# Feed-forward operands without 1/rms for the early batches alone, then rebuilt from DRAM

## The chip, the cores and the metric

The kernel runs on one core of a Trainium2 chip. The metric is device microseconds of one execution. Five engines work side by side: PE (matrix products; PEld are its weight loads), DVE (element-wise work), ACT (functions and copies), POOL (element-wise work, SBUF only) and SP, whose queue issues all the DMAs of this kernel. PE's clock is granted at one of two levels, 2.4 or 1.2 GHz.

## The reference, cut to what matters

Two layers; each is a token mixer followed by a SwiGLU feed-forward block, S = 1024 tokens, D = 1024, F = 2816:

```python
h = rms_norm(x, ffn_norm_g[layer])       # x * rsqrt(mean(x*x) + eps) * g
a = einsum('bsd,df->bsf', h, w_gate)
u = einsum('bsd,df->bsf', h, w_up)
x = x + einsum('bsf,fd->bsd', silu(a) * u, w_down)
```

The change lies in the two gate-and-up stages, `a` and `u`.

## The kernel before, in words

Tokens lie along the free dimension, in two halves `th` of 512; features lie on the 128 partitions. Every float32 product is made of three PE matmuls on operands split into a rounded high part and a rest (ACT casts, DVE subtracts): `split` (L1058) for weights, `split2` (L1051) for activations, whose instructions stand at L102 (ACT) and at L1062 and L1055 (DVE).

`feed_forward` (L1333) runs once for each layer. It ends the output projection in `out_rest` (L972), once for each half: 48 matmuls (L374 to L376), DVE adds the residual (L988), the sum is stored to `y_dram`, squared and added up, and scaled by the norm's gain. At its end stands `rms` (L329): DVE adds two partial sums (L334), ACT and DVE split them, two matmuls (L339, L340) give the mean square, and ACT and DVE make 1/rms, `rt`, of that half.

The gate-and-up stage multiplies by a seven-product scheme (Strassen's, in Winograd's form). Its right operands `B[0]` to `B[6]` are sums of the four quarters of the scaled activations. Products 0 and 1 use quarters of the first half alone: `B[0]` and `B[1]` are split before that half's 1/rms is known. Hence the results of products 0 and 1 must be multiplied by `rt` afterwards. `B[2]` to `B[6]` contain 1/rms; `rights_late` (L1022) makes them, `times_r` (L1007) multiplying a quarter by `rt`.

The weights come in 11 batches of two feature blocks each. In `todo` products 0 and 1 of the first three batches (EARLY) come first, then their products 2 to 6, then batches 3 to 10 with all seven. `prep_gate` (L1078) makes a product's weights three or four products ahead (POOL forms sums at L1089 to L1093, then `split`); `gate` (L1108) runs 24 matmuls (L1120 to L1122), 12 in each of two PSUM banks. Products 0 and 1 go to the same bank, as do 2 and 3, and 4 and 5: the matmuls of product 1 may start only when the bank's value after product 0 has been read. In an early batch ACT copies that value (L1133, L1138) and DVE multiplies later (L1145). In a late batch:

```python
nc.vector.tensor_tensor(v["p"], ps, self.rt[:, 0:TH], ALU.mult)   # L1135, product 0
nc.vector.tensor_tensor(v["s"], ps, self.rt[:, 0:TH], ALU.mult)   # L1140, product 1
self.S.activation(v["s"], v["s"], AF.Silu)                        # L1141
```

Product 2 is read by DVE at L1149, 3 at L1151, 4 at L1155, 5 at L1158, 6 at L1162. After product 6 POOL multiplies (L1163) and `hidden` (L1169) forms four DVE sums (L1175 to L1178) and stores seven parts (L1180).

Places: `Slots` hands out fixed SBUF places, first freed first used; in this stage 44 places of 1024 columns hold activations, operands, raw weights and split weights together. The gate weights of batches 1 and 2 are given up after their first use (L1101) and loaded again (`take_raw`, L1070). Who runs when on each engine is decided at build time by a scheduler that goes by program order and by when it takes an instruction to be ready; each engine then works its list in order.

Of the kernel before, what the change touches and what calls it, by code (L numbers as in the profile page):

```python
# [18 lines left out]
P = 128  # L19
D = 1024  # L20
S = 1024
# [95 lines left out]
class Trunk:  # L117
    def __init__(self, ctx, tc, a, out):
# [13 lines left out]
        self.p_dram = [dr.tile([P, S], F32, name=f"pd{i}") for i in range(KC)]  # L132
        self.y_dram = [dr.tile([P, S], F32, name=f"yd{i}") for i in range(KC)]
        self.t_dram = [dr.tile([P, 7 * TH], F32, name=f"td{i}") for i in range(NF // 2)]
        self.c_dram = dr.tile([8, S], F32, name="cd")
# [836 lines left out]
    def out_rest(self, l, th, w, acc, gain):  # L972


        nc = self.nc
        sl = slice(th * TH, th * TH + TH)

        def scale(k):
            x = self.x_at(k, th)
            self.S.activation(x, x, AF.Copy, scale=self.gains[:, gain + k:gain + k + 1])  # L980

        for k in range(KC):
            ps = self.rF.get()
            c = slice(k * P, k * P + P)
            self.mm3(ps[:], [y[2][:, 0, c] for y in w], [y[3][:, 0, c] for y in w],
                     [r32(t[:, sl]) for t in self.oH[6:]], [r32(t[:, sl]) for t in self.oL[6:]])
            x = self.x_at(k, th)
            nc.vector.tensor_tensor(x, ps[:], x, ALU.add)  # L988
            nc.sync.dma_start(self.y_dram[k][:, sl], x)
            self.squares(acc, x, k, k < 2)  # L990
            if k >= 3:
                scale(k - 3)
        for k in range(KC - 3, KC):
            scale(k)
        x = self.xt
        if th == 0:
            for t in range(4):
                self.B[t // 2].append(self.split2(x[t]))
            self.rms(acc, th)
            for m in range(2):  # L1000
                self.times_r(x[m], 0)
        else:
            self.rms(acc, th)
            for m in range(2):
                nc.vector.tensor_tensor(x[4 + m][:], x[6 + m][:], x[4 + m][:], ALU.subtract)
# [16 lines left out]
    def rights_late(self):  # L1022
# [20 lines left out]
        for m in range(2):  # L1043
            self.times_r(x[2 + m], 0)
            v.tensor_tensor(x[2 + m][:], x[2 + m][:], x[m][:], ALU.subtract)
# [24 lines left out]
    def take_raw(self, b, which=(0, 1)):  # L1070

        for w in which:
# [3 lines left out]
            self.raws[b, w] = t  # L1076

    def prep_gate(self, b, i):  # L1078
        p = self.nc.gpsimd
        out = []  # L1080
        for n in range(2):
            g = self.raws[b, 0][n]
            a11, a12 = g[:, 0:TH], g[:, TH:2 * TH]
            if i >= 2:
                u = self.raws[b, 1][n]
                a21, a22 = u[:, 0:TH], u[:, TH:2 * TH]
            if i == 2:
                s1 = self.tmp[n] = self.hf.get()
                p.tensor_tensor(s1[:], a21, a22, ALU.add)  # L1089
                p.tensor_tensor(a21, a11, a21, ALU.subtract)  # L1090
                p.tensor_tensor(a11, s1[:], a11, ALU.subtract)
            if i == 5:
                p.tensor_tensor(a12, a12, a11, ALU.subtract)  # L1093
            out.append(self.split((a11, a12, a11, None, None, a12, None)[i] if i not in (3, 4, 6) else
                                  a21 if i == 3 else self.tmp[n][:] if i == 4 else a22))
            if i == 4:
                self.hf.put(self.tmp[n])
            if i == 6:
                self.sf.put(g, u)
        if i == 1 and 0 < b < self.EARLY:  # L1100
            self.sf.put(*self.raws[b, 0])  # L1101
        if b < self.EARLY and i in (4, 6):
            self.take_raw(b + 1, (1,) if i == 4 else (0,))
        elif self.EARLY <= b < self.BATCHES - 1 and i == 1:
            self.take_raw(b + 1)
        return out

    def gate(self, b, i, W):  # L1108
# [3 lines left out]
        for n in range(2):  # L1112
# [4 lines left out]
            for j in range(4):  # L1117
# [3 lines left out]
                nc.tensor.matmul(ps, wh, bl, start=False, stop=False, skip_group_check=True)  # L1121
                nc.tensor.matmul(ps, wl, bh, start=False, stop=j == 3, skip_group_check=True)  # L1122
            self.sr.put(w)
            v = self.v[b][n]
            if i == 0:
# [3 lines left out]
                else:  # L1129
                    v["hp"], v["hs"] = self.hf.get(), self.hf.get()  # L1130
                    v["p"], v["s"] = v["hp"][:], v["hs"][:]
                if b < self.EARLY:
                    self.S.copy(v["p"], ps)  # L1133
                else:
                    nc.vector.tensor_tensor(v["p"], ps, self.rt[:, 0:TH], ALU.mult)  # L1135
            elif i == 1:
                if b < self.EARLY:
                    self.S.copy(v["s"], ps)  # L1138
                else:
                    nc.vector.tensor_tensor(v["s"], ps, self.rt[:, 0:TH], ALU.mult)  # L1140
                    self.S.activation(v["s"], v["s"], AF.Silu)  # L1141
            elif i == 2:
# [18 lines left out]
            else:  # L1161
                nc.vector.tensor_tensor(v["p"], ps, v["p"], ALU.add)  # L1162
                nc.gpsimd.tensor_tensor(v["s"], v["s"], v["p"], ALU.mult)  # L1163
        if b == self.BATCHES - 1:
            self.sr.put(*(x for hl in self.B[i] for x in hl))
        if i == 6:
            self.hidden(b)
# [165 lines left out]
    def feed_forward(self, l):  # L1333
# [3 lines left out]
        self.B = [[] for _ in range(7)]  # L1337
        self.raws, self.v, self.ps, self.tmp = {}, {}, [None, None], [None, None]
        self.wd, self.rights, self.keep_sums = {}, deque(), {}
# [32 lines left out]
        self.sr.put(*self.oH[6:], *self.oL[6:])  # L1372
        self.sf.put(acc)
        late = self.rights_late()
        for m, (_, run) in enumerate(todo):
# [7 lines left out]
            run(made[m])  # L1383
            made[m] = None
            if 2 <= m < 7:
                next(late)
# [145 lines left out]
```

## Time and profile before

| | us |
|---|---|
| median of three runs | 2624.08 (2619.69 to 2624.88) |
| the profiled execution | 2617.69 |
| its span, first to last instruction | 2615.9 |
| PE busy in it | 2464.0 |
| DVE busy | 1959.6 |
| ACT busy | 1284.9 |
| POOL busy | 884.9 |
| first layer's gate-and-up stage, about | 663 to 1130 |
| second layer's, about | 1937 to 2402 |

Busy times are sums over instructions. PE's matmuls overlap one another, so a busy PE is not PE at its peak; idle time in front of a matmul, with the engine that ended it, says more. A row of a timeline gives the start, the duration, the engine, the line and, in brackets, the idle time before it and who ended that.

### The profile page before, as it was taken

What the parts mean: (1) busy time and instruction counts of PE and PEld (TensorE: products, weight loads), DVE (VectorE), ACT (ScalarE), POOL (GpSimd) and SP (SyncE); (2) the same over time, 40 slices, a digit from 0 to 9 for tenths busy, and PEclk for the clock granted to TensorE, in tenths of its full rate; (3) what the DMA queues carried; (4) which work ended last, traced back from release to release, by engine and by line L of the source; (5) the groups of instructions that cost most, each with busy time, mean ns of one, the idle gap of its engine ahead of it and who ended that gap; (6) DMA issues with size and microseconds to landing.
All of it is one profiled execution on the core that took longest, in us unless ns stands there. A gap on an engine that the chain in (4) does not pass through costs nothing.

```text
span 2615.9 us, 34843 instructions
## 1 busy us (share of the span) xinstructions
PE 2464.0 (94%) x11896; PEld 2020.6 (77%) x11896; DVE 1959.6 (75%) x3359; ACT 1284.9 (49%) x2578; POOL 884.9 (34%) x696
## 2 busy tenths in 40 slices
PE   8898899999889999999999999998988999999999
PEld 7786778777767777788878877776776777778887
DVE  7969958897976665689576687778779666566974
ACT  5646667764622222344466576666564222233352
POOL 4111111120355443366142232323233534333920
PEclk9999999999999999999999999999999999999999
DMA  5323142464133222375333232334422322317462
GB/s 182 90 49 89 29 107 77 117 205 168 57 119 124 92 104 93 128 264 156 109 126 83 68 99 63 97 85 134 165 107 77 136 93 89 113 69 274 129 186 83
DMA packets 147117, 303.30 MB, mean 116 GB/s; under 512 B 18387, under 2 KB 24308, under 8 KB 146940
## 3 DMA queue, kind: packets, MB, share of 16 engines
q1 hardware_dynamic: 146940, 301.09, 37.0%
q8 instruction: 93, 1.52, 0.3%
q14 instruction: 84, 0.69, 0.1%
HBM read 187.74 MB, written 71.34 MB: 99 GB/s over the span
## 4 chain that ended last, share of the span: by engine, by line
PE 55%; DVE 20%; issue 9%; POOL 7%; ACT 6%; DMA 2%; SPq 0%; POOLq 0%; DVEq 0%; ACTq 0%
PE bk L1260 5%; PE bk L1262 5%; PE bk L1261 5%; PE bk L375 4%; PE bk L376 4%; PE bk L374 4%; PE bk L1120 4%; PE bk L1121 4%; PE bk L1122 4%; PE bk L690 4%; DVE sr L1062 3%; PE bk L568 3%; DVE sf L586 3%; PE bk L676 2%; ACT sr L102 2%
## 5 line engine op out<-in xcount | busy, mean ns | idle before, releaser
L102 ACT CAST sr<-sf 128x512 fp32r<-128x512 f32 (+2 forms) x516 | 323.1, 643 | 594.1 <-PE bk L1122 301.5
L1120 PE MATMUL bk<-sr,sr 128*128 128x512 f32 x1232 | 487.7, 396 | 51.1 <-DVE hf L1135 31.3
L1121 PE MATMUL bk<-sr,sr 128*128 128x512 f32 x1232 | 484.9, 394 | 0.0
L1122 PE MATMUL bk<-sr,sr 128*128 128x512 f32 x1232 | 484.1, 393 | 0.0
L1062 DVE TENSOR_TENSOR sr<-sf,sr 128x512 fp32r<-128x512 f32 x426 | 390.0, 923 | 88.1 <-ACT sr L102 85.3
L1120 PEld LDWEIGHTS bk<-sr,sr 128*128 128x128 f32 x1232 | 234.6, 190 | 109.6 <-DVE hf L1135 36.3
L374 PE MATMUL bk<-sr,sr 128*128 128x512 f32 x768 | 307.0, 400 | 3.0 <-ACT sr L102 2.8
L375 PE MATMUL bk<-sr,sr 128*128 128x512 f32 x768 | 305.6, 398 | 2.4 <-DVE sr L931 2.3
L376 PE MATMUL bk<-sr,sr 128*128 128x512 f32 x768 | 304.5, 397 | 0.0
L220 POOL TENSOR_TENSOR sr<-raw,sr 128x512 fp32r<-128x512 f32 (+2 forms) x140 | 191.4, 1383 | 302.9 <-ACT sr L102 167.6
L1122 PEld LDWEIGHTS bk<-sr,sr 128*128 128x128 f32 x1232 | 234.6, 190 | 49.4
L1121 PEld LDWEIGHTS bk<-sr,sr 128*128 128x128 f32 x1232 | 235.1, 191 | 48.1
L102 ACT CAST sr<-hf 128x512 fp32r<-128x512 f32 (+1 forms) x260 | 161.1, 620 | 194.0 <-PE bk L1122 67.6
L1261 PE MATMUL bk<-sr,sr 128*128 128x512 f32 x616 | 239.8, 389 | 0.6 <-DVE sr L1062 0.6
L1262 PE MATMUL bk<-sr,sr 128*128 128x512 f32 x616 | 239.7, 389 | 0.0
L1260 PE MATMUL bk<-sr,sr 128*128 128x512 f32 x616 | 239.6, 389 | 0.0
L1062 DVE TENSOR_TENSOR sr<-hf,sr 128x512 fp32r<-128x512 f32 x190 | 202.8, 1070 | 23.5 <-ACT sr L102 22.7
L568 PE MATMUL bk<-sr,sr 128*128 128x512 f32 (+2 forms) x768 | 200.5, 360 | 7.9 <-ACT sf L110 6.5
L690 PE MATMUL bk<-hr,sr 128*128 128x512 f32 (+2 forms) x560 | 165.5, 388 | 13.6 <-DVE hr L708 11.0
L102 ACT CAST hr<-bk 128x512 fp32r<-128x512 f32 (+2 forms) x240 | 122.5, 525 | 104.1 <-PE bk L676 91.5
L708 DVE TENSOR_TENSOR hr<-bk,hr 128x512 fp32r<-128x512 f32 (+2 forms) x240 | 142.2, 603 | 41.4 <-ACT hr L102 40.0
L374 PEld LDWEIGHTS bk<-sr,sr 128*128 128x128 f32 x768 | 145.4, 190 | 31.8 <-ACT sr L102 3.8
(203 smaller groups left out, 4942.0 us busy)
## 6 DMA issues: line engine op xcount, KB each, us to landing
hf<-td SPq DMA_DIRECT2D x146, 256.0 KB, 3.0
td<-hf SPq DMA_DIRECT2D x138, 256.0 KB, 2.0
sf<-in_wg_dram SPq DMA_DIRECT2D x52, 512.0 KB, 3.3
sr<-sr SPq DMA_DIRECT2D x96, 256.0 KB, 3.3
sf<-in_wu_dram SPq DMA_DIRECT2D x44, 512.0 KB, 3.3
sf<-in_wd_dram SPq DMA_DIRECT2D x88, 256.0 KB, 5.2
raw<-in_w_dram SPq DMA_DIRECT2D x64, 256.0 KB, 2.9
sr<-sr SPq DMA_DIRECT2D x128, 128.0 KB, 2.3
```

The costliest lines, as they stand in the source:

```text
L102: self.last = self.e.copy(out, in_)
L374: nc.tensor.matmul(ps, WH[k], hH[k], start=first and k == 0, stop=False)
L375: nc.tensor.matmul(ps, WH[k], hL[k], start=False, stop=False)
L376: nc.tensor.matmul(ps, WL[k], hH[k], start=False, stop=last and k == n - 1)
L568: nc.tensor.matmul(b[:, 0:hi - lo], r32(Q[i // 4][:, q]), r32(KK[:, lo:hi]), start=j == 0, stop=j == 1)
L1062: self.nc.vector.tensor_tensor(r32(t[:, TH:2 * TH]), x, t[:, 0:TH], ALU.subtract)
L1120: nc.tensor.matmul(ps, wh, bh, start=i in (0, 2, 4, 6) and j == 0, stop=False, skip_group_check=True)
L1121: nc.tensor.matmul(ps, wh, bl, start=False, stop=False, skip_group_check=True)
L1122: nc.tensor.matmul(ps, wl, bh, start=False, stop=j == 3, skip_group_check=True)
L1260: nc.tensor.matmul(ps, wh, bh, start=i in (0, 6, 2, 4) and j == 0, stop=False, skip_group_check=True)
L1261: nc.tensor.matmul(ps, wh, bl, start=False, stop=False, skip_group_check=True)
L1262: nc.tensor.matmul(ps, wl, bh, start=False, stop=j == self.PAIRS - 1, skip_group_check=True)
```

## The change

- For the early batches `B[0]` and `B[1]` stay without 1/rms. The first half's four scaled tiles are all multiplied by `rt` in `out_rest` and stored in a new DRAM buffer, `h_dram`.
- After products 0 and 1 of batch 2 the places of `B[0]` and `B[1]` are given up. Behind products 3 and 4 of that batch the tiles are loaded again and split into new `B[0]` and `B[1]`, now with 1/rms.
- In the late batches ACT copies product 0 from PSUM and applies Silu to product 1 straight from PSUM; DVE's two multiplications by `rt` are gone.
- The second half's `rms` moves from the end of `out_rest` to behind product 1 of batch 0; its PE instructions are held behind that product's last matmul.
- POOL's three sums of a batch become a step of their own, `sums_gate`, issued earlier: for batch 0 at the preparation of product 0 of batch 1, for batches 1 and 2 at product 5 of the batch before, for the late ones at their own product 1.
- The gate weights of batches 1 and 2 stay in their places until their product 6, and are not loaded twice.

```diff
--- before.py
+++ after.py
@@ -131,6 +131,7 @@
         self.x_dram = [dr.tile([P, S], F32, name=f"xd{i}") for i in range(KC)]
         self.p_dram = [dr.tile([P, S], F32, name=f"pd{i}") for i in range(KC)]
         self.y_dram = [dr.tile([P, S], F32, name=f"yd{i}") for i in range(KC)]
+        self.h_dram = [dr.tile([P, S], F32, name=f"hd{i}") for i in range(4)]
         self.t_dram = [dr.tile([P, 7 * TH], F32, name=f"td{i}") for i in range(NF // 2)]
         self.c_dram = dr.tile([8, S], F32, name="cd")
         self.b_dram = [dr.tile([P, 384], F32, name=f"bd{h}") for h in range(8)]
@@ -997,10 +998,10 @@
             for t in range(4):
                 self.B[t // 2].append(self.split2(x[t]))
             self.rms(acc, th)
-            for m in range(2):
+            for m in range(4):
                 self.times_r(x[m], 0)
+                nc.sync.dma_start(self.h_dram[m][:], x[m][:])
         else:
-            self.rms(acc, th)
             for m in range(2):
                 nc.vector.tensor_tensor(x[4 + m][:], x[6 + m][:], x[4 + m][:], ALU.subtract)
 
@@ -1041,7 +1042,6 @@
         self.sf.put(*x[6:8])
         yield
         for m in range(2):
-            self.times_r(x[2 + m], 0)
             v.tensor_tensor(x[2 + m][:], x[2 + m][:], x[m][:], ALU.subtract)
             self.B[6].append(self.split2(x[2 + m]))
             self.sf.put(x[m], x[2 + m])
@@ -1074,6 +1074,17 @@
             for x, f in zip(t, (2 * b, 2 * b + 1)):
                 self.nc.sync.dma_start(x[:].rearrange("p (k c) -> p k c", k=8), self.a["wg" if w == 0 else "wu"][self.l, f])
             self.raws[b, w] = t
+
+    def sums_gate(self, b):
+
+        p = self.nc.gpsimd
+        for n in range(2):
+            (a11, a21), a22 = (self.raws[b, w][n][:, 0:TH] for w in range(2)), self.raws[b, 1][n][:, TH:2 * TH]
+            s1 = self.tmp[b, n] = (self.sf if b == 0 else self.hf).get()
+            s1 = s1[:, 0:TH]
+            p.tensor_tensor(s1, a21, a22, ALU.add)
+            p.tensor_tensor(a21, a11, a21, ALU.subtract)
+            p.tensor_tensor(a11, s1, a11, ALU.subtract)
 
     def prep_gate(self, b, i):
         p = self.nc.gpsimd
@@ -1084,23 +1095,21 @@
             if i >= 2:
                 u = self.raws[b, 1][n]
                 a21, a22 = u[:, 0:TH], u[:, TH:2 * TH]
-            if i == 2:
-                s1 = self.tmp[n] = self.hf.get()
-                p.tensor_tensor(s1[:], a21, a22, ALU.add)
-                p.tensor_tensor(a21, a11, a21, ALU.subtract)
-                p.tensor_tensor(a11, s1[:], a11, ALU.subtract)
             if i == 5:
                 p.tensor_tensor(a12, a12, a11, ALU.subtract)
             out.append(self.split((a11, a12, a11, None, None, a12, None)[i] if i not in (3, 4, 6) else
-                                  a21 if i == 3 else self.tmp[n][:] if i == 4 else a22))
+                                  a21 if i == 3 else self.tmp[b, n][:, 0:TH] if i == 4 else a22))
             if i == 4:
-                self.hf.put(self.tmp[n])
+                (self.sf if b == 0 else self.hf).put(self.tmp.pop((b, n)))
             if i == 6:
                 self.sf.put(g, u)
-        if i == 1 and 0 < b < self.EARLY:
-            self.sf.put(*self.raws[b, 0])
-        if b < self.EARLY and i in (4, 6):
-            self.take_raw(b + 1, (1,) if i == 4 else (0,))
+        due = 0 if (b, i) == (1, 0) else b + 1 if b + 1 < self.EARLY and i == 5 else b if b >= self.EARLY and i == 1 else None
+        if due is not None:
+            self.sums_gate(due)
+        if b + 1 < self.EARLY and i == 3:
+            self.take_raw(b + 1, (1,))
+        elif b + 1 == self.EARLY and i in (4, 6):
+            self.take_raw(b + 1, (0,) if i == 4 else (1,))
         elif self.EARLY <= b < self.BATCHES - 1 and i == 1:
             self.take_raw(b + 1)
         return out
@@ -1119,7 +1128,8 @@
                 bh, bl = (r32(x[:, j % 2 * TH:j % 2 * TH + TH]) for x in self.B[i][j // 2])
                 nc.tensor.matmul(ps, wh, bh, start=i in (0, 2, 4, 6) and j == 0, stop=False, skip_group_check=True)
                 nc.tensor.matmul(ps, wh, bl, start=False, stop=False, skip_group_check=True)
-                nc.tensor.matmul(ps, wl, bh, start=False, stop=j == 3, skip_group_check=True)
+                last = nc.tensor.matmul(ps, wl, bh, start=False, stop=j == 3, skip_group_check=True)
+            self.pe_last = last.ins
             self.sr.put(w)
             v = self.v[b][n]
             if i == 0:
@@ -1129,16 +1139,12 @@
                 else:
                     v["hp"], v["hs"] = self.hf.get(), self.hf.get()
                     v["p"], v["s"] = v["hp"][:], v["hs"][:]
-                if b < self.EARLY:
-                    self.S.copy(v["p"], ps)
-                else:
-                    nc.vector.tensor_tensor(v["p"], ps, self.rt[:, 0:TH], ALU.mult)
+                self.S.copy(v["p"], ps)
             elif i == 1:
                 if b < self.EARLY:
                     self.S.copy(v["s"], ps)
                 else:
-                    nc.vector.tensor_tensor(v["s"], ps, self.rt[:, 0:TH], ALU.mult)
-                    self.S.activation(v["s"], v["s"], AF.Silu)
+                    self.S.activation(v["s"], ps, AF.Silu)
             elif i == 2:
                 if b < self.EARLY:
                     for x in ("p", "s"):
@@ -1161,8 +1167,15 @@
             else:
                 nc.vector.tensor_tensor(v["p"], ps, v["p"], ALU.add)
                 nc.gpsimd.tensor_tensor(v["s"], v["s"], v["p"], ALU.mult)
-        if b == self.BATCHES - 1:
+        if b == self.BATCHES - 1 or i < 2 and b == self.EARLY - 1:
             self.sr.put(*(x for hl in self.B[i] for x in hl))
+            self.B[i] = []
+        if b == self.EARLY - 1 and i in (3, 4):
+            for m in (0, 1) if i == 3 else (2, 3):
+                t = self.sf.get()
+                nc.sync.dma_start(t[:], self.h_dram[m][:])
+                self.B[i - 3].append(self.split2(t))
+                self.sf.put(t)
         if i == 6:
             self.hidden(b)
 
@@ -1335,7 +1348,7 @@
         nc = self.nc
         self.l = l
         self.B = [[] for _ in range(7)]
-        self.raws, self.v, self.ps, self.tmp = {}, {}, [None, None], [None, None]
+        self.raws, self.v, self.ps, self.tmp = {}, {}, [None, None], {}
         self.wd, self.rights, self.keep_sums = {}, deque(), {}
         self.nblk = self.nright = self.n3 = self.n4 = 0
         if 6 not in self.loaded:
@@ -1370,7 +1383,6 @@
         for x in w:
             self.sr.put(x[0], x[1])
         self.sr.put(*self.oH[6:], *self.oL[6:])
-        self.sf.put(acc)
         late = self.rights_late()
         for m, (_, run) in enumerate(todo):
             s = m - gates
@@ -1382,6 +1394,10 @@
             prep_to(m + (3 if m < 7 * self.EARLY else 4 if s < 0 else 5))
             run(made[m])
             made[m] = None
+            if m == 1:
+                with self.tc.issue_after(self.pe_last):
+                    self.rms(acc, 1)
+                self.sf.put(acc)
             if 2 <= m < 7:
                 next(late)
             if l == 0 and (n - 12 <= s < n - 4 or s == n - 1):
```

## Rows read from the trace of the kernel before

**Rows 1.** The page's first part: busy time, share and count of each engine

```profile
PE 2464.0 (94%) x11896; PEld 2020.6 (77%) x11896; DVE 1959.6 (75%) x3359; ACT 1284.9 (49%) x2578; POOL 884.9 (34%) x696
```

**Rows 2.** Waits of PE, whole span: us in total, times, longest

```profile
PE bk L1120 <- DVE hf L1135: 31.3, 15, 2.2
PE bk L1120 <- DVE hf L1149: 18.6, 4, 8.9
PE bk L339 <- ACT hr L102: 15.6, 3, 6.8
```

**Rows 3.** Timeline of the turn to batch 4, 851 to 855 us

```profile
851.51 1.64 POOL L1163 TENSOR_TENSOR hf<-hf,hf 128x512 f32<-128x512 f32 x1 [1.23 <-DVE hf L1162]
851.98 0.39 PE L1122 MATMUL bk<-sr,sr 128*128 128x512 f32 x1
...
853.19 0.69 DVE L1178 TENSOR_TENSOR hf<-hf,hf 128x512 f32<-128x512 f32 x1 [1.16 <-POOL hf L1163]
853.80 0.68 DVE L1135 TENSOR_TENSOR hf<-bk,rt 128x512 f32<-128x512 f32 x1
...
854.54 0.50 PE L1120 MATMUL bk<-sr,sr 128*128 128x512 f32 x1 [2.17 <-DVE hf L1135]
```

**Rows 4.** Stretches: us, PE, PEld, DVE, ACT, POOL busy (count), clock, DMA

```profile
668.00:753.00 85.00, 68.00 (x284) 54.63 (x283) 84.44 (x84) 40.99 (x64) 39.36 (x23) 0.91 0.17 59
753.00:812.00 59.00, 56.78 (x239) 45.73 (x237) 35.67 (x48) 14.36 (x24) 35.23 (x25) 0.96 0.43 148
...
853.00:894.00 41.00, 38.37 (x168) 31.45 (x168) 25.97 (x33) 11.16 (x19) 17.02 (x13) 1.00 0.27 97
...
1012.00:1052.00 40.00, 37.83 (x161) 30.80 (x160) 23.58 (x32) 11.00 (x18) 14.78 (x12) 0.96 0.26 92
...
2230.00:2270.00 40.00, 37.83 (x160) 30.89 (x159) 25.01 (x32) 11.15 (x18) 16.83 (x12) 0.96 0.25 91
```

**Rows 5.** Timelines of the first layer's early stretch, DVE, then PE

```profile
671.89 4.55 DVE L1011 TENSOR_TENSOR sf<-sf,rt 128x1024 f32<-128x1024 f32 x2
...
680.24 1.74 DVE L334 TENSOR_TENSOR sf<-sf 128x512 f32<-128x512 f32 x1
...
693.75 2.35 DVE L1011 TENSOR_TENSOR sf<-sf,rt 128x1024 f32<-128x1024 f32 x2
...
682.68 0.80 PE L339 MATMUL bk<-hr,sub 128*128 128x512 f32 x1 [6.77 <-ACT hr L102]
...
751.89 0.80 PE L1120 MATMUL bk<-sr,sr 128*128 128x512 f32 x1 [8.86 <-DVE hf L1149]
```

**Rows 6.** ACT's and DVE's instructions by form, 676 to 1120: busy, mean ns

```profile
L102 ACT CAST sr<-sf 128x1024 fp32r<-128x1024 f32 x10 | 10.4, 1054 | 2.7 <-DVE sf L1045 2.3 <-DVE sf L1035 0.3
L102 ACT COPY sf<-bk 128x512 f32<-128x512 f32 x8 | 4.7, 586 | 2.8 <-PE bk L1122 2.7
...
L1055 DVE TENSOR_TENSOR sr<-sf,sr 128x1024 fp32r<-128x1024 f32 x10 | 12.2, 1262 | 0.0
...
L1140 DVE TENSOR_TENSOR hf<-bk,rt 128x512 f32<-128x512 f32 x16 | 11.0, 690 | 6.5 <-PE bk L1122 6.5
L1135 DVE TENSOR_TENSOR hf<-bk,rt 128x512 f32<-128x512 f32 x16 | 10.9, 683 | 0.1
```

**Rows 7.** Waits of ACT, 812 to 1000 us

```profile
ACT sr L102 <- PE bk L1122: 91.6, 30, 9.9
```

**Rows 8.** Stretch 666 to 676, PE alone: us, busy (count), clock, DMA

```profile
666.00:676.00 10.00, 9.92 (x44) 1.00 0.28 101
```

**Rows 9.** DMA issues: count, KB each, median us to landing

```profile
sf<-in_wg_dram SPq DMA_DIRECT2D x52, 512.0 KB, 3.3
...
sf<-od SPq DMA_DIRECT2D x14, 512.0 KB, 4.4
```

**Rows 10.** Chain of work that ended last, 660 to 860: start, us, what

```profile
723.71 3.21 DMA sf<-in_wg_dram
...
733.55 1.63 POOL sf L1091
```

## The prediction

> **What bounds the kernel now.** The first look is at the busy shares: PE is busy for 94% of the span, DVE for 75%, ACT for 49% [rows 1]. So PE sets the time, and a change pays by idle time of PE that it removes, or by a lower clock that it avoids. The second look is at PE's waits over the whole span [rows 2]. The three longest entries lie in the stage that the change touches. The first is 31.3 us in 15 waits for L1135, the multiplication of product 0 by rt. The second is 18.6 us in four waits for L1149, two of them long. The third is 15.6 us, nearly all of it for the matmul of the second half's norm (L339). Together that is 65.5 us, 2.5% of the time, and they have different causes.
>
> *Late batches.* The third look is at a timeline where one batch ends and the next begins [rows 3]. PE ends product 0's first bank at 852.0. DVE, which works its list in order, stands at L1178, and that waits for POOL's L1163 until 853.2. L1135 follows at 853.8, and PE resumes at 854.5 after 2.17 us. DVE is not short of time here, with 26.0 of 41 us busy [rows 4]; it is held up by the batch before.
>
> *The early stretch.* Between 668 and 753 DVE is busy for 84.4 of 85 us [rows 4]. Here DVE is the bound, and PE's idle time only shows where PE meets it: 6.8 us at L339 and 8.9 us at L1120 [rows 5]. The second layer repeats it.
>
> I cost against the profiled execution, 2617.7 us, whose span is 2615.9. The median of the runs is 6.4 us longer, and I carry that difference over.
>
> **The change part by part.**
>
> *Product 0 and 1 of the late batches.* Removed are 32 L1135 and 32 L1140, 0.683 and 0.690 us each [rows 6] (sixteen of each in the first layer), 44 us of DVE that is mostly not on the path. Added are 32 copies on ACT at 0.586 us, the time of the same copy in the early batches [rows 6]. Silu changes only its source; its cost stays between nothing and the copy's time more, hidden by ACT's idle time of about 30 us per batch [rows 4]. The copy doesn't stand behind L1178. It has the 2.7 us of the other bank's matmuls to finish in: 24 matmuls take 38.4/168 x 24 = 5.5 us [rows 4]. So the 31.3 us go, all of them. The bounds are 0 and 31.3. I take the upper end since the early batches already run the same copy between products 0 and 1, and no PE wait for it is among the long ones. If ACT's cover fails, the copy waits behind casts: ACT does wait 91.6 us for PE to free places in 812 to 1000 [rows 7], and a copy behind two such casts would cost PE some of the 2.17 us again.
>
> Two of these waits are followed by a stretch at a mean clock of 0.96 [rows 4] (from 1012 and from 2230), so PE ran for a time at 1.2 GHz. 40 x 0.04 = 1.6 us each; without the waits about 3 us come back. Late sum: 34 us.
>
> *The second norm behind product 1.* In the ten microseconds before the wait PE already runs 44 matmuls, nearly all of products [rows 8]. That is almost the two products (48) behind which the change puts the norm. The scheduler had moved it there of its own accord. The wait itself comes from L334, which DVE reaches only at 680.2 [rows 5], behind multiplications by rt that take 2.3 us each beside a working POOL and 1.2 us without it [rows 5] (at 671.9 and at 693.8). Two of the four L1011 of the first half move ahead of the norm in program order; one of them ran there already. So this step alone is worth between -2.3 us (one more slow L1011 in front) and 6.8 us, per layer.
>
> *POOL's sums earlier, gate weights kept.* Eight of the 52 loads of gate weights go [rows 9]. In the chain of waits one such load, 3.2 us at 723.7, is followed by POOL's sums until 735.2 and then by DVE's splits [rows 10]. With the weights at hand the sums can run some ten microseconds earlier, and DVE need not work around them. The number of POOL's sums and of DVE's instructions stays.
>
> *The whole early stretch.* Since DVE is the bound, its parts can't be added up. Where the wait at L339 shrinks and the one at L1120 grows by as much, it is 0; the lower end is the slow L1011 that moves ahead, -2.3 us. The upper end is both waits gone, 6.8 + 8.9 us, with the clock that falls after each, 59 x 0.04 = 2.4 us [rows 4] (the stretch from 753): in all about 20.5 us per layer. I take 4 us per layer, nearer the lower end, because DVE's 0.6 us of idle time [rows 4] are the only slack that a better order can use directly; the rest must come from fewer DVE instructions slowed by POOL. Early sum: 8 us.
>
> The Trainium skill (SBUF — State Buffer, Who interferes with whom) says that a DVE instruction with two SBUF inputs and a POOL instruction that reads SBUF exclude each other, whichever starts first. By that rule moving POOL's sums moves their price along and the early sum would be 0; the doubled L1011 agree with it.
>
> *Rebuilding B[0] and B[1].* Per layer: four stores and four loads of 512 KB, four casts at 1.05 us, four subtractions at 1.26 us [rows 6], 4.2 us of ACT and 5.0 us of DVE. They fall in the third early batch, in a stretch where DVE is busy 35.7 and ACT 14.4 of 59 us [rows 4]. Issued behind products 3 and 4 of batch 2 they have two to four products (11 to 22 us) until batch 3. A load of 512 KB from DRAM lands in 4.4 us [rows 9] (the attention output), so load, cast and subtraction take about 7 us: hidden, 0. Were they wholly exposed it would be 7 us per layer, 14 in all. The eight stores and eight loads take the places of eight loads of weights on SP's queue; the stores wait there for L1011, with only the residual sums and weights issued later behind them.
>
> *Sum.* 31.3 + 3 + 8 - 0 = 42 us. 2617.7 - 42 = 2575.7; with 6.4 us, **2582 us**.
>
> **The rivals.**
>
> *A, the early stretch gives nothing.* For it: DVE has no slack, and the same instructions and the same POOL work remain. Against it: some sums can leave the crowded time. Only the late 34 us go: 2590 us. Chance 0.25.
>
> *B, both early waits go.* For it: the chain passes through a load and sums that move away. Against it: 84.4 of 85 us. 34 + 41 = 75 us: 2549 us. Chance 0.12.
>
> *C, the copy inherits the wait.* ACT's list is in order too, and if casts for later weights stand in front of the copy, PE keeps about half of the 2.17 us. For it: ACT's 91.6 us of waiting for places [rows 7]. Against it: program order has the copy ahead of the later casts. 2582 + 17 = 2599 us. Chance 0.09.
>
> *D, slower: the places run out.* Counting hand-outs, no place is free when the second weights of batch 1 are asked for, so that load waits for a split of B[4], and that for PE to end product 0 of batch 2. Split (2.3 us), load (3.3), POOL's sums (about 8) and the next split (3) make some 17 us, and PE has six products, 33 us, until it needs the result. The slack is 16 us. It decides from 16 us of delay on, and then takes the early sum too: 2590 + 2 x (delay - 16). The kernel is slower from about 36 us on; at 40 us, more than twice the chain, the time would be 2590 + 48 = 2638 us. Chance 0.03.
>
> *E, no change.* A and C together, and the rebuilt operands wholly exposed: 2590 + 17 + 14 = 2621 us. Each is unlikely, and all three would have to hold. Chance 0.04.
>
> **How the numbers follow.** My forecast, 2582 with 2575 to 2588, has 0.47. The range takes in A and C, and leaves out D, E and B: 2558 to 2604. A measurement of this kernel can tell about 0.2%, 5.2 us, from no change. The forecast, A, B and C lie on the faster side, 0.93; I keep 0.90, since all share the claim that late waits vanish. Same is 0.05, slower 0.05.
>
> **What would show it.** In PE's waits L1135 must be gone and no ACT copy in its place; a late batch must take about 38.3 us, not 40.5. The stretch after the output projection must still show DVE busy without a gap, and PE's waits there, L339 and L1149, should sum to 12 to 16 us per layer, not to 3. POOL's sums of batch 1 should run before 725. The first matmul of batch 3 should not wait. I'm wrong if a late batch still shows 2 us of idle PE, if the early waits are gone, or if products 0 and 1 of batch 3 wait for the rebuilt operands.

## The result and the profile after

The changed kernel takes 2596.63 us (median; 2594.32 to 2599.55), the kernel before, run beside it, 2624.33: a ratio of 0.9899 [0.9882, 0.9916]. That is 27.7 us less by the medians and 26.5 us by the ratio, which goes by the means. The forecast was 2582, 14.6 us lower, with a range from 2558 to 2604. The profiled executions lie closer together, 2599.55 against 2617.69, since one is the slowest run of its kernel and the other lies below every timed run of its own.

The page's busy times of the changed kernel, which answer to [rows 1]:

```profile
PE 2467.1 (95%) x11896; PEld 2021.0 (78%) x11896; DVE 1912.1 (74%) x3303; ACT 1300.8 (50%) x2618; POOL 902.3 (35%) x696
```

DVE has lost 47.5 us, ACT has gained 15.9. Lines of the changed kernel stand a few higher: L1129 to L1131 are the matmuls L1120 to L1122 of before; L1155, L1161 and L1164 read products 2, 4 and 5 (L1149, L1155, L1158 before); L340 is the norm's matmul L339; L1012 is `times_r`; L1085 to L1087 are POOL's sums; L1166 and L1169 are POOL's products (L1160, L1163), L1191 the last DVE sum (L1178).

PE's waits over the whole span (us in total, times, longest), those of the changed stage, beside [rows 2]:

```profile
PE bk L1129 <- DVE hf L1155: 18.0, 9, 7.2
...
PE bk L1129 <- DVE hf L1161: 9.1, 4, 2.9
...
PE bk L1129 <- ACT hf L102: 4.9, 2, 2.7
PE bk L340 <- ACT hr L102: 4.8, 4, 2.1
PE bk L375 <- DVE sf L989: 3.4, 4, 1.0
...
PE bk L1131 <- DVE sr L1062: 3.4, 2, 1.7
```

The 31.3 us of L1135 are gone, and so is most of the norm's 15.6. The wait for product 2 (18.6 before) has not moved, and four smaller entries are new or larger (L1161, L989, L1062, and two waits for ACT's copy).

Stretches of the changed kernel (columns as in [rows 4]):

```profile
668.00:753.00 85.00, 72.73 (x306) 58.11 (x306) 78.44 (x92) 48.77 (x78) 35.01 (x20) 0.97 0.28 98
753.00:812.00 59.00, 54.67 (x221) 43.92 (x222) 36.89 (x47) 16.68 (x25) 28.50 (x20) 0.93 0.39 136
...
850.00:900.00 50.00, 49.99 (x221) 41.04 (x220) 31.27 (x38) 15.17 (x26) 24.91 (x18) 1.00 0.31 112
...
2230.00:2270.00 40.00, 39.99 (x176) 32.78 (x176) 23.78 (x29) 12.34 (x21) 19.03 (x14) 1.00 0.29 100
```

In both late stretches shown, 850 to 900 and 2230 to 2270, PE is busy without a gap, at 2.4 GHz; 2230 to 2270 held 160 matmuls at a mean clock of 0.96 before [rows 4] and holds 176 now. In the early stretch the two rows together hold 527 matmuls, against 284 + 239 = 523 before [rows 4]. So the whole gain is late, and the early stretch as a whole has not become faster. Timeline of the turn to batch 4, all but PE's rows:

```profile
852.35 1.67 POOL L1169 TENSOR_TENSOR hf<-hf,hf 128x512 f32<-128x512 f32 x1 [1.41 <-DVE hf L1168]
...
856.37 0.59 ACT L102 COPY hf<-bk 128x512 f32<-128x512 f32 x1 [2.10 <-PE bk L1131]
...
858.19 1.67 POOL L1169 TENSOR_TENSOR hf<-hf,hf 128x512 f32<-128x512 f32 x1 [1.23 <-DVE hf L1168]
859.09 0.59 ACT L102 COPY hf<-bk 128x512 f32<-128x512 f32 x1 [1.61 <-PE bk L1131]
...
859.89 0.69 DVE L1191 TENSOR_TENSOR hf<-hf,hf 128x512 f32<-128x512 f32 x1 [1.18 <-POOL hf L1169]
```

DVE still stands at its last sum, waiting for POOL [rows 3]. But both copies have run on ACT before that sum starts, and PE waits for nothing.

The early stretch of the first layer, rows of three timelines (PE, then DVE, then POOL), beside [rows 5]:

```profile
686.88 0.49 PE L340 MATMUL bk<-hr,sub 128*128 128x512 f32 x1 [0.33 <-ACT hr L102]
...
729.07 0.50 PE L1129 MATMUL bk<-sr,sr 128*128 128x512 f32 x1 [2.91 <-DVE hf L1161]
...
753.36 0.79 PE L1129 MATMUL bk<-sr,sr 128*128 128x512 f32 x1 [6.92 <-DVE hf L1155]
...
819.15 0.80 PE L1129 MATMUL bk<-sr,sr 128*128 128x512 f32 x1 [2.65 <-ACT hf L102]
...
676.98 5.72 DVE L1012 TENSOR_TENSOR sf<-sf,rt 128x1024 f32<-128x1024 f32 x4
...
646.11 1.33 POOL L1085 TENSOR_TENSOR sf<-sf 128x512 f32<-128x512 f32 x1 [24.12 <-PE bk L377]
```

POOL's sums of batch 0 start at 646; before, at 669.8. The four L1012 ahead of the norm take 1.4 us each on average (5.72/4) where [rows 5] had 2.3, and the wait at the norm falls from 6.77 to 0.33. In its place stand waits of 1 to 3 us, and the long one for product 2 stays.

### The profile page after: what moved, and what is told of

Same layout as the page of the kernel before. It is cut to its first block, busy times and chain, and to the rows that moved or that the text cites. A ratio compares the mean times of both kernels' runs of the same rounds, so it can differ in the third digit from the quotient of the medians.

```text
span 2597.6 us, 34806 instructions
## 1 busy us (share of the span) xinstructions
PE 2467.1 (95%) x11896; PEld 2021.0 (78%) x11896; DVE 1912.1 (74%) x3303; ACT 1300.8 (50%) x2618; POOL 902.3 (35%) x696
## 4 chain that ended last, share of the span: by engine, by line
PE 64%; DVE 17%; ACT 6%; POOL 5%; issue 5%; DMA 2%; SPq 0%; DVEq 0%; POOLq 0%; ACTq 0%
PE bk L1129 8%; PE bk L1130 8%; PE bk L1131 8%; PE bk L1275 5%; PE bk L1273 5%; PE bk L1274 5%; PE bk L376 4%; PE bk L375 4%; PE bk L377 4%; PE bk L691 4%; PE bk L569 3%; DVE sf L587 3%; PE bk L677 2%; ACT sf L110 2%; DVE sr L1062 2%
## 5 line engine op out<-in xcount | busy, mean ns | idle before, releaser
L102 ACT CAST sr<-sf 128x512 fp32r<-128x512 f32 (+2 forms) x528 | 331.8, 648 | 559.0 <-PE bk L1131 189.0
L1129 PE MATMUL bk<-sr,sr 128*128 128x512 f32 x1232 | 487.8, 396 | 32.2 <-DVE hf L1155 18.0
L1062 DVE TENSOR_TENSOR sr<-sf,sr 128x512 fp32r<-128x512 f32 x430 | 411.2, 963 | 121.5 <-ACT sr L102 119.8
L1131 PE MATMUL bk<-sr,sr 128*128 128x512 f32 x1232 | 483.9, 393 | 3.4 <-DVE sr L1062 3.4
L1129 PEld LDWEIGHTS bk<-sr,sr 128*128 128x128 f32 x1232 | 234.4, 190 | 91.9 <-DVE hf L1155 26.5
L1131 PEld LDWEIGHTS bk<-sr,sr 128*128 128x128 f32 x1232 | 234.2, 190 | 53.6 <-DVE sr L1062 4.2
L1062 DVE TENSOR_TENSOR sr<-hf,sr 128x512 fp32r<-128x512 f32 x186 | 188.2, 1021 | 27.4 <-ACT sr L102 26.8
```

The source lines that it names most:

```text
L102: self.last = self.e.copy(out, in_)
L1062: self.nc.vector.tensor_tensor(r32(t[:, TH:2 * TH]), x, t[:, 0:TH], ALU.subtract)
L1129: nc.tensor.matmul(ps, wh, bh, start=i in (0, 2, 4, 6) and j == 0, stop=False, skip_group_check=True)
L1131: last = nc.tensor.matmul(ps, wl, bh, start=False, stop=j == 3, skip_group_check=True)
```

## The experiments

Each ratio is to the kernel before on the same chip; the changed kernel's is 0.9899. A thousandth is 2.6 us.

### One part alone, one part undone

**Late part and rebuilding alone** (norm, sums and loads as before), the late-only kernel:

```diff
-            for m in range(2):
+            for m in range(4):
                 self.times_r(x[m], 0)
+                nc.sync.dma_start(self.h_dram[m][:], x[m][:])
...
-                if b < self.EARLY:
-                    self.S.copy(v["p"], ps)
-                else:
-                    nc.vector.tensor_tensor(v["p"], ps, self.rt[:, 0:TH], ALU.mult)
+                self.S.copy(v["p"], ps)
```

> The kernel before with one part of the change: operands rebuilt from DRAM, late batches read from PSUM by ACT; the norm, POOL's sums and the double load of gate weights as before. Theory 1 (the gain is the late batches' 31 us of waits and some 3 us of clock; DVE bounds the early stretch, so the norm and the sums bring nothing): no wait for the late copies, PE's early waits about 38 us as before, 2590 to 2600 us. Rival (the norm behind the products and the earlier sums are worth 8 us or more each, and the rebuilding eats some of the late gain): 2605 us or more.

Measured: 0.9961 [0.9948, 0.9973], only 9.2 us. The late waits are gone, but in the first layer's early stretch the wait at the norm has grown from 6.8 to 9.2 us, and waits for a weight's split (5.0) and for Silu (3.0) are new; the wait for product 2 has fallen from 9.3 to 4.6 (the 3.0 us may belong to it, as shown below). The time lies in the rival's range. The growth at the norm is what the forecast's lower end names: one more slow L1011 in front of it, 2.3 us.

**The norm put back** at the end of `out_rest`:

```diff
         else:
+            self.rms(acc, th)
```

> The changed kernel with the second half's norm back at the end of the output projection. Theory 1: PE's wait at the norm's matmul comes back with 6 to 7 us per layer, and the waits for product 2 of batch 1 (L1155) shrink by nearly as much; within 5 us of the changed kernel's 2596.6. Rival: the norm's wait is a loss of its own, 2609 us or more.

Measured: 0.9917 [0.9903, 0.9930]. The difference, 5 us, lies inside the intervals, but the waits didn't go as Theory 1 has it: in the first layer the one at the norm comes back with 3.9 us only, and the one for product 2 grows, from 8.7 to 11.9 us.

**The sums put back** at product 2 of their batch:

```diff
+            if i == 2:
+                s1 = self.tmp[b, n] = self.hf.get()
+                p.tensor_tensor(s1[:], a21, a22, ALU.add)
...
-        if due is not None:
-            self.sums_gate(due)
```

> The changed kernel with POOL's three sums back at the preparation of product 2, gate weights still kept. Theory 1: within 5 us of 2596.6, since POOL's and DVE's work in the early stretch stays the same. Rival (earlier sums help): 2604 us or more. A third reading (the sums of batch 1 now collide with DVE between 714 and 726, where one of POOL's took 6.9 us): 2592 us or less.

Measured: 0.9968 [0.9957, 0.9980], 0.0069 or 18 us worse than the changed kernel. DVE's row and PE's, from two timelines:

```profile
672.93 9.02 DVE L1012 TENSOR_TENSOR sf<-sf,rt 128x1024 f32<-128x1024 f32 x4
...
690.39 0.80 PE L340 MATMUL bk<-hr,sub 128*128 128x512 f32 x1 [8.93 <-ACT hr L102]
```

Beside POOL's sums (670.8 to 689.1) the four L1012 take 2.26 us each again, and the wait at the norm is 8.93 us, although the norm still stands behind product 1. Moving the sums emptied most of this wait: with the sums moved and the norm put back it was 3.9 us. It is not the only one that returns; PE also waits 6.6 us for a weight's split and 7.1 us for the read of product 4 (L1163 here).

**DVE copies product 0** in the late batches:

```diff
-                self.S.copy(v["p"], ps)
+                if b < self.EARLY:
+                    self.S.copy(v["p"], ps)
+                else:
+                    nc.vector.tensor_copy(v["p"], ps)
```

> The changed kernel with product 0 of the late batches copied by DVE instead of ACT, as many DVE instructions as it takes for that alone; everything else as changed. Theory 1 (what cost time was DVE's in-order wait for POOL in front of that read, not the length of DVE's work): 2.2 us per late batch come back, 32 to 36 us in all, 2626 to 2634 us. Rival (DVE's 44 us of multiplications were the cost): only the 22 us of copies return to an engine with slack, 2597 to 2605 us.

Measured: 1.0014 [1.0005, 1.0023]. The first row of PE's waits over its whole span, L1145 being the copy:

```profile
PE bk L1129 <- DVE hf L1145: 25.0, 12, 2.2
```

The wait of 2.2 us is back as soon as the read stands on DVE's list, whatever the operation. In the late batches the place on DVE's list costs, not the multiplication.

**The late part without rebuilding:** the kernel before with ACT's copy and Silu in the late batches and nothing else.

```diff
-                    nc.vector.tensor_tensor(v["s"], ps, self.rt[:, 0:TH], ALU.mult)
-                    self.S.activation(v["s"], v["s"], AF.Silu)
+                    self.S.activation(v["s"], ps, AF.Silu)
```

> The kernel before, with nothing changed but that ACT copies product 0 of the late batches and applies Silu to product 1 from PSUM; their multiplication by 1/rms is left out, so this times the late part alone, without rebuilt operands, stores or moved work. Theory 2 (the late part is worth its whole 34 us, and the early stretch takes some 25 us of it away in the late-only kernel): 0.985 to 0.989 of before, about 2583 to 2593 on this chip's scale, early waits of PE 17 to 18 us per layer as before. Rival (the late part was worth only the 9 us that the late-only kernel shows): 0.995 or more.

Measured: 0.9894 [0.9881, 0.9908], 27.7 us: the price of the late part by itself. Against 34 us forecast, 4.8 us went into a wait for ACT's copy, once per layer, that the changed kernel shows too (4.9 us). ACT's rows in the changed kernel, at the turn to batch 3:

```profile
818.00 0.62 ACT L102 CAST sr<-sf 128x512 fp32r<-128x512 f32 x1 [6.22 <-DVE sf L1191]
818.52 0.58 ACT L102 COPY hf<-bk 128x512 f32<-128x512 f32 x1
```

ACT's list has a cast that waits for DVE's last sum of batch 2 in front of the copy. That is rival C, once per layer.

### Can the early stretch be made better?

**Two of the four multiplications left in the last operand step:**

```diff
-            for m in range(4):
+            for m in range(2):
                 self.times_r(x[m], 0)
...
+            self.times_r(x[2 + m], 0)
+            self.nc.sync.dma_start(self.h_dram[2 + m][:], x[2 + m][:])
```

> The changed kernel, with the multiplications of the two further first-half tiles by rt, and their stores, left where the kernel before had them, in the last step of the late operands. Theory 2a (the two multiplications ahead of the norm delay the whole early chain on DVE): PE's early waits fall by 2 to 5 us per layer, 4 to 10 us faster than the changed kernel, 0.986 to 0.989 of before. Rival 2b (it is the rebuilding and the places, not these multiplications): within 3 us of the changed kernel, 0.989 to 0.991.

Measured: 0.9969 [0.9957, 0.9981], 18 us worse than the changed kernel. Neither theory forecast that. The trace shows that the edit moved little: the scheduler still runs three of the four multiplications ahead of the norm, as in the kernel before, and the fourth at 687.4. PE now waits 8.2 us in the first layer for casts of weights, and 3.9 us for a split. ACT's casts ahead of the longest of these waits begin at 728.2, when a late one of POOL's sums (L1089) is done; in the changed kernel they begin at 725.4. Why the order on ACT's list differs is not shown.

**The results' places of batch 2 handed out a product later,** so that no cast stands in front of the copy:

```diff
-                self.sf.put(v["both"])
+                if b == self.EARLY - 1:
+                    self.held.append(v["both"])
...
-            prep_to(m + (3 if m < 7 * self.EARLY else 4 if s < 0 else 5))
+            prep_to(m + (3 if m <= 7 * self.EARLY else 4 if s < 0 else 5))
...
+            if m == 7 * self.EARLY:
+                self.sf.put(*self.held)
```

> The changed kernel, with the places that hold batch 2's results handed out one product later, so that no cast of weights that waits for them can stand in front of ACT's copy of batch 3's product 0. Theory: the wait of 2.3 to 2.7 us per layer for that copy goes, with the clock that falls behind it (up to 2.4 us); 4 to 10 us faster than the changed kernel, 0.986 to 0.988 of before. Rival (PE then waits for DVE or for the rebuilt operands at the same turn): 0.989 to 0.990.

Measured: 0.9912 [0.9897, 0.9927], no gain. Another cast that waits for the same sum took the place in front of the copy, and PE's wait stayed at 2.3 us in the first layer.

**Two early batches** (`EARLY = 2`):

> The changed kernel with two early batches instead of three: four multiplications by rt less on DVE per layer in the early stretch, two products less to cover the second half's norm. If DVE's amount of work bounds the early stretch: PE's early waits fall by 3 to 5 us per layer, 6 to 10 us faster, 0.986 to 0.988 of before. If the chain from the norm to the first operand with 1/rms bounds it: PE arrives 10.9 us earlier per layer and waits for it, slower by 8 us or more, 0.993 or more.

Measured: 0.9972 [0.9963, 0.9981], 19 us worse. The norm's wait is back at 6.4 us in the first layer, with 4.4 us for a cast, 3.6 at the norm's second matmul and 5.2 for L989 in the output projection. That is the second reading's time: there is less to do, but PE reaches what it waits for sooner. The wait for L989, ahead of the products, is not explained by it.

**The second weights of batch 1 and their sums earlier:**

```diff
+        if (b, i) == (1, 1):
+            self.take_raw(1, (1,))
...
+        due = 0 if (b, i) == (1, 0) else 1 if (b, i) == (2, 1) else b + 1 if 0 < b < self.EARLY - 1 and i == 5 else
```

> The changed kernel with the second weights of batch 1 asked for at the preparation of product 1 of batch 1, six products' preparations earlier, and POOL's sums of that batch at product 1 of batch 2, when POOL is idle. Theory 3 (in the changed kernel the sums of batch 1 start only when that load lands at 713.7, and are then held up by DVE, one of them for 6.9 us; ACT's casts, DVE and PE stand behind them): PE's early waits fall by 4 to 8 us per layer, 8 to 16 us faster than the changed kernel, 0.984 to 0.987 of before. Rival (DVE's amount of work bounds the stretch wherever the sums stand): 0.988 to 0.992.

Measured: 0.9946 [0.9934, 0.9958], 12 us worse. A DVE row, then a PE row:

```profile
679.82 9.02 DVE L1012 TENSOR_TENSOR sf<-sf,rt 128x1024 f32<-128x1024 f32 x4
...
697.30 0.79 PE L340 MATMUL bk<-hr,sub 128*128 128x512 f32 x1 [7.52 <-ACT hr L102]
```

The sums moved out of 714 to 733 and into 678 to 696, beside the operands of the norm. L1012 takes 2.26 us again and the wait at the norm is back. When POOL works decides, and earlier is not better.

### What the rebuilding costs

**Late part, moved multiplications and stores, but nothing rebuilt:**

```diff
-            self.B[i] = []
-        if b == self.EARLY - 1 and i in (3, 4):
...
-                self.B[i - 3].append(self.split2(t))
```

> The late-only kernel without the rebuilding: B[0] and B[1] keep their places and stay without 1/rms, so the late batches' products 0 and 1 leave that factor out; the four multiplications and stores at the end of the first half stay. The late-only kernel stands at 0.9961, ACT reading alone at 0.9894. If the loads, casts, subtractions and handed-back places of the rebuilding cost the 17 us between them: about 0.990. If the moved multiplications and the stores do: about 0.996.

Measured: 0.9904 [0.9888, 0.9919]. It is 0.0010 from the late part without rebuilding (0.9894), so moving two multiplications ahead of the norm and adding four stores, per layer, costs some 3 us, inside the intervals. It is 0.0057 from the late-only kernel (0.9961): loading, splitting and handing back places cost 15 us. The late-only kernel has the wait for Silu (L110) at 764, since DVE comes to batch 2's multiplications later:

```profile
764.40 0.47 PE L1121 MATMUL bk<-sr,sr 128*128 128x512 f32 x1 [3.01 <-ACT sf L110]
...
761.91 1.74 DVE L1142 TENSOR_TENSOR sf<-sf,rt 128x512 f32<-128x512 f32 x1
763.58 0.68 DVE L1146 TENSOR_TENSOR hf<-bk,sf 128x512 f32<-128x512 f32 x1
764.18 2.85 DVE L1142 TENSOR_TENSOR sf<-sf,rt 128x512 f32<-128x512 f32 x2
```

The multiplications shown (L1142) are the last three of batch 2; without rebuilding all four are done by 754.7. Here DVE splits later weights (L1063) in between, beside POOL's sums for them. The profile puts the wait down to Silu, but DVE's read of product 2 (L1146), which frees the bank, ends only 0.06 us before Silu; both stand behind the multiplication at 761.9. The mean clock around the wait is 0.81, so that some 10 of the 27 us were at 1.2 GHz (27 x 0.19 / 0.5). The stretch in both kernels, first with rebuilding, then without (columns as in [rows 4]):

```profile
753.00:780.00 27.00, 21.09 (x74) 16.56 (x75) 22.05 (x24) 7.49 (x12) 14.46 (x10) 0.81 0.18 61
```

```profile
753.00:780.00 27.00, 25.89 (x106) 20.99 (x107) 17.70 (x24) 7.17 (x12) 13.96 (x10) 0.93 0.34 114
```

Over the longer stretch from 668 to 900 the late-only kernel ends 36 matmuls behind (856 against 892). At 38.4/168 us each [rows 4] that is 8.2 us in the first layer, about half of the 15. PE is busy only 2.9 us less there (206.6 against 209.5 us), so by these rows the larger part of the 8.2 is the lower clock (0.94 against 0.96 over the 232 us), not waiting.

**Places handed back later:** as the late-only kernel, but the places of `B[0]` and `B[1]` go back right before the loads that rebuild them.

```diff
         if b == self.EARLY - 1 and i in (3, 4):
+            self.sr.put(*(x for hl in self.B[i - 3] for x in hl))
+            self.B[i - 3] = []
```

> The late-only kernel with one thing moved: the places of B[0] and B[1] are handed back right before the loads that rebuild them (behind products 3 and 4 of batch 2), not behind products 0 and 1. Loads, casts and subtractions stay. Theory 1: the rebuilding's price of some 15 us comes from the places being handed back early, which lets splits of later weights run ahead of the multiplications and of the second weights of batch 2. Then it falls away here: about 2596 us, as without the rebuilding, and the wait of 3.0 us for ACT's Silu at 764 and the low clock behind it are gone. Theory 2: the price is that of the loads, casts and subtractions themselves (9 us of ACT and DVE per layer in a stretch that has none to spare). Then the time stays at 2609 to 2613 us, as in the late-only kernel.

Measured: 0.9959 [0.9945, 0.9973], as slow as the late-only kernel, which is Theory 2's time. Theory 1 had the place right: batch 2's last multiplication is back at 754, the wait for Silu is gone, and the stretch from 753 to 780 holds 99 matmuls, where the late-only kernel has 74 and the one without rebuilding 106. The time is not back, though. A row of DVE, one of PE, then three of ACT:

```profile
754.46 0.68 DVE L1142 TENSOR_TENSOR sf<-sf,rt 128x512 f32<-128x512 f32 x1
...
823.96 0.79 PE L1121 MATMUL bk<-sr,sr 128*128 128x512 f32 x1 [7.85 <-ACT hf L102]
...
810.70 0.59 ACT L102 COPY hf<-bk 128x512 f32<-128x512 f32 x1 [0.77 <-PE bk L1123]
820.72 0.62 ACT L102 CAST sr<-sf 128x512 fp32r<-128x512 f32 x1 [9.43 <-DVE sf L1183]
...
823.33 0.58 ACT L102 COPY hf<-bk 128x512 f32<-128x512 f32 x1
```

and in the kernel without rebuilding:

```profile
814.03 0.50 PE L1121 MATMUL bk<-sr,sr 128*128 128x512 f32 x1 [2.70 <-ACT hf L102]
...
812.87 0.62 ACT L102 CAST sr<-sf 128x512 fp32r<-128x512 f32 x1 [6.27 <-DVE sf L1175]
```

The casts and subtractions of the rebuilding now lie between 790 and 803, ahead of the end of batch 2; DVE's last sum comes at 819 instead of 812. ACT's cast waits for that sum, the second copy waits behind the cast, and PE waits 7.85 us instead of 2.70. In both kernels the work finds no free place on DVE's and ACT's lists; only the wait in which it shows changes.

### The late wait by its cause

**Only DVE's last sum held back** behind the next batch's first multiplication, in the kernel before:

```diff
-        nc.vector.tensor_tensor(t4, b21, t2, ALU.subtract)
+        with self.tc.issue_after(self.first) if self.first is not None else ExitStack():
+            nc.vector.tensor_tensor(t4, b21, t2, ALU.subtract)
```

The edit also issues a batch's whole step `hidden` behind that multiplication. On DVE's list the other three sums still run ahead of it (at the turn shown by this trace from 885.7 to 892.2, the multiplication at 893.4, the last sum at 894.7).

> The kernel before, with one order changed: in the late batches the last of DVE's four sums of a batch (the one that waits for POOL) is held behind the first multiplication by rt of the next batch; DVE still multiplies, nothing is rebuilt. If the late waits are only a matter of DVE's order: they go, and the time is that of ACT reading alone, 0.988 to 0.991 of before. If the length of DVE's work matters too: PE then waits for the second bank's multiplication, 0.993 or more.

Measured: 0.9949 [0.9937, 0.9962], 11.3 us. Two rows of PE's waits over the span; L1154 reads product 2:

```profile
PE bk L1120 <- DVE hf L1154: 27.0, 18, 8.9
...
PE bk L1120 <- DVE hf L1135: 8.1, 14, 2.2
```

L1135 falls by 23.2 us, and the wait for product 2 rises by 8.4 [rows 2]. The order on DVE's list alone is worth under half of what ACT's copy gains, so the length of the list counts too: the wait moves on to the next read, at product 2.

None of these kernels that computes the whole is faster than the changed one.

## Why the prediction was right or wrong

*Late batches: right in mechanism, 6 us too high.* The wait comes from DVE's list: it returns with a DVE copy as with the multiplication, and goes with ACT's copy. (The row at 851.98 [rows 3], which the prediction takes for the end of product 0's first bank, is the last matmul of its second; the first was full at 849.7, 4.1 us before DVE read it.) The forecast took the upper end of the bound, 31.3 + 3 = 34; measured alone it is 27.7. The step that failed is "The copy doesn't stand behind L1178": true for seven turns of a layer, false for the turn to batch 3, where a cast that waits for batch 2's last sum stands in front of the copy (4.8 us in two layers). Rival C was priced for every batch; it came once per layer.

*Rebuilding: the mis-sized term.* "Hidden, 0" was wrong; the kernels that differ in it alone give 15 us, about the other bound, 14, though not by the load, cast and subtraction in a row that this bound stands for. The cover was named as DVE's and ACT's idle time between 753 and 812, 35.7 and 14.4 of 59 us busy [rows 4]. That is an average over a stretch. With the places handed back early, POOL's sums and the splits of later weights fill its beginning, ahead of batch 2's multiplications; with the places handed back late, the casts and subtractions themselves stand just ahead of the last sum of batch 2. PE waits for either, and part of the price is the lower clock behind such waits.

*The early order: about twice the term, not zero.* From the late-only kernel to the changed one the ratio falls by 0.0062, 16 us, against 8 forecast, nearly all from the earlier sums (18 us with the rest in place; the norm's 5 is not clear of the intervals, and keeping the gate weights was not undone by itself). The forecast's reason held: fewer DVE instructions slowed by POOL. L1012 takes 1.4 or 2.26 us according to whether POOL's sums run beside it. That agrees with the rule of the Trainium skill (SBUF — State Buffer, Who interferes with whom) that the two exclude each other. Not borne out is what the prediction drew from it, that the price only moves along. Part of it does: at 646 to 668 there are now 2.9 us of waits in the output projection and the first norm that were not there. But a third of DVE's work there is L989, which reads PSUM (6.4 of 20.5 us busy) and keeps its 0.68 us, while the splits L1062 rise from 0.68 to 1.2. That less waits for DVE there is argued, not shown.

*The sum.* 27.7 - 3 - 15 + 16 = 26 us. The last three terms are differences along one chain of kernels, from the late part alone to the changed kernel, so they must add up to the ratio's 26.5 us; the sum doesn't test them. Rebuilding and early order cancel, so the time lies between rivals A's (2590) and C's (2599) for another reason than either's: the early stretch didn't give nothing, it gave 16 and paid 18. That the time fell into the range is in part luck, since a cost put at nothing was met by a gain put at half.

*The checks named beforehand.* L1135 is gone and late batches run without idle PE: right. POOL's sums of batch 1 were to run before 725; the last of the three ends at 731.4: wrong. They start only when the second weights land at 713.7, and DVE then holds one up. The first matmul of batch 3 was not to wait; it waits 2.65 us: wrong. The early waits L340 and product 2 sum to 1.5 + 8.7 = 10.2 us in the first layer, not 12 to 16, but with the new small ones to 22.

*Not settled:* that splits come before multiplications goes with the places handed back early, since handing them back late undoes it; but single instructions of the rebuilding were not left out one by one, so its 15 us are not divided among loads, casts and subtractions.

## What to carry to other kernels

A read that frees a PSUM bank belongs on an engine whose list holds no wait for other work in front of it; the order of the list counts first (DVE's copy cost PE the same 2.2 us a turn as its multiplication), and its length after that (order alone gave 11.3 of 27.7 us). Work that is called hidden needs a gap at its place in that list, and a stretch's mean busy time doesn't show one. Where POOL and DVE meet, decide which DVE instructions POOL may slow: those that nothing waits for soon.

## What the hardware showed

POOL can be starved as well as slow DVE. Two rows of POOL in the changed kernel and those of DVE beside the first:

```profile
716.74 6.87 POOL L1086 TENSOR_TENSOR sf<-sf,sf 128x512 f32<-128x512 f32 x1
...
727.82 1.72 POOL L1086 TENSOR_TENSOR sf<-sf,sf 128x512 f32<-128x512 f32 x1
```

```profile
716.63 2.34 DVE L1045 TENSOR_TENSOR sf<-sf,sf 128x1024 f32<-128x1024 f32 x2
718.90 0.68 DVE L1062 TENSOR_TENSOR sr<-sf,sr 128x512 fp32r<-128x512 f32 x1
719.50 2.35 DVE L1055 TENSOR_TENSOR sr<-sf,sr 128x1024 fp32r<-128x1024 f32 x2
721.77 0.68 DVE L1062 TENSOR_TENSOR sr<-sf,sr 128x512 fp32r<-128x512 f32 x1
722.37 1.27 DVE L1157 TENSOR_TENSOR hf<-bk,hf 128x512 f32<-128x512 f32 x2
```

The same operation takes 6.87 us and 1.72; POOL's times are rough, but the kernel with the norm put back shows it again (6.86 us). DVE works without a gap on two SBUF inputs and keeps its full speed (1.2 us per 1024 columns). The sum ends at 723.61, 1.24 us after the start of DVE's first instruction that reads a PSUM bank. That is about what a sum takes alone (1.3 us, L1085 at 646.11), so it seems to have got nowhere until then. Beside the slow L1012, 2.26 us each, POOL's sums took up to 2.28 us, so there both gave way. What decides between the two is not shown.
